# The output projection of a transformer block: retention rows, residual tiles and the gate in another place and order

## The chip, the cores and the metric

The kernel runs on one core of one Trainium2 chip. The metric is the device time of one execution in microseconds; for the kernel before it is 2900.07 us, the median of three runs (2897.08 to 2903.02).

## The reference

Two blocks are computed in float32. The change lies in the first, between its mixers and its feed-forward stage.

```python
# one block of the first stage (DEPTH = 1); D_MODEL = 1024, SEQ = 1024, D_FF = 4096
x = layer_norm(x, ln_in_g, ln_in_b)
mod = silu(c) @ w_ada + b_ada
sh1, sc1, gt1, sh2, sc2, gt2 = split(mod, 6)
h = x * (1.0 + sc1) + sh1
proj = h @ w_in                     # q_c, kv_c, k_r for the attention; r_q, r_k, r_v, r_g for the retention
a = mla_mixer(q_c, kv_c, k_r, ...)                  # 512 columns
r = retention_mixer(r_q, r_k, r_v, r_g, ...)        # 512 columns, 4 heads, a norm per row and head, a gate from r_g
y = concatenate([a, r], -1) @ w_out
x = layer_norm(ALPHA * x + gt1 * y, ln1_g, ln1_b)
h = x * (1.0 + sc2) + sh2
f = square(relu(h @ w_ff1)) @ w_ff2
x = layer_norm(ALPHA * x + gt2 * f, ln2_g, ln2_b)
# a second block follows (differential attention, gated linear attention, cross attention, mixture of experts)
```

## The kernel before

The sequence of 1024 rows is cut into eight tiles of 128 rows (t = 0 to 7), and for the matmuls into two halves of four tiles. Float32 products are made of three matmuls on pairs of a rounded value and its residual (hi and lo): mm3 (L194) issues hi x hi, hi x lo and lo x hi, one matmul each at L197, L198 and L199. A product of 128 rows, 1024 inner and 512 outer columns is 24 matmuls into one PSUM bank. Weights come as pieces of 128x1024 into a raw buffer (DMA, L160), ScalarE rounds them (L164, whi), DVE subtracts (L165, wlo). Three raw buffers and five pairs of hi and lo turn round; the output projection has three more pairs (xwh, xwl).

The order of each engine is set when the program is built: the code is written in the order below, and a scheduler then orders each engine's instructions by when their operands are expected and by the priority of the code's order. Buffers of a pool are handed on when their last reader is done, and a pool that opens where another closed waits for the last users of the old memory.

Before the change the stage runs as follows. retain (L820) walks the retention's eight tiles: loads of qk and v, transposes, the scan, the output rows r (L779), their statistics. After every fourth tile the statistics give a reciprocal root, and 16 activations on ScalarE (L795) norm four rows. Between the tiles gate_cols (L798) computes the gate's columns with the projection of the input, 24 matmuls each. ret_half (L809) transposes four rows (L250), applies the group gain on ScalarE (L815, u), the gate on DVE (L816) and splits the result into the left operand of the output projection (L817, L818); for rows 0 to 3 it stands after the sixth tile, for rows 4 to 7 at the end.

out_proj (L858) loads the gate gt1 over all partitions, and the gain and bias of the input norm (ling, linb), scaled by ALPHA on DVE (L866). For each tile it loads x, norms it (L869, DVE), multiplies by ling (L870, DVE) and adds linb (L871, POOL): that is the residual acc. gemm_resident (L212) multiplies with both column halves of w_out resident: tiles 0 to 3 for columns 0 to 511, the same tiles for columns 512 to 1023, then tiles 4 to 7 with both halves in turn. Four PSUM banks hold results; the evacuation multiplies by gt1 (L877, from PSUM, DVE) and adds to acc (L878, DVE). When a tile has both halves, done (L901) takes its statistics, norms it (L904, DVE), and after four tiles mod_half (L461) transposes them into the operand of the feed-forward stage, and POOL applies ALPHA times ln1's gain and bias to acc (L908, L909).

feed_forward (L917) has eight chunks of 512 hidden columns. In a chunk eight up products of 24 matmuls are followed by relu (ScalarE, L940), the square (DVE, L942), rounding (ScalarE, L943, hidh) and residual (DVE, L944); then 16 down products with weights that POOL has multiplied by gt2 (L996), which DVE adds to acc (L1007).

## Time and profile before

| what | value |
|---|---|
| median of three runs | 2900.07 us (2897.08 to 2903.02) |
| profiled execution | 2900.44 us |
| its span | 2898.6 us |
| mean granted clock of TensorE | 0.976 of full speed |
| TensorE, DVE, ScalarE, POOL busy | 95%, 63%, 47%, 16% of the span |
| stage of the change | some 430 to 735 us of the span |

Times are counted from the span's start. PE is TensorE, ACT is ScalarE, POOL is GpSimd, SP the engine that issues the loads. An idle time in brackets is that of the engine before the instruction, and the arrow names what ended it. Matmuls are pipelined, so the distance of two starts tells their pace, and not the duration that is printed. The granted clock is given in parts of full speed (2.4 GHz).

### The profile page before, as it was taken

The numbers are of one execution on the slowest core, as the hardware profiler recorded it, in microseconds if no ns is written. First come the engines' busy times: TensorE is split into PE (matmuls) and PEld (weight loads), VectorE is DVE, ScalarE is ACT, GpSimd is POOL, SyncE is SP. The second block draws the span as 40 slices with busy tenths as digits, with TensorE's granted clock in tenths as the row PEclk, the third lists the DMA queues.
The fourth block names the chain that finished last, engine by engine and source line by source line (L and its number), as shares of the span: only waits on it lengthen the run. The fifth ranks groups of instructions, "written<-read, shape, count | busy, mean of one in ns | idle before, by whom it ended". The sixth has DMA issues, their size and how long they took to land. (4 is left out here: it accounts for less than half of the span.)

```text
span 2898.6 us, 36767 instructions
## 1 busy us (share of the span) xinstructions
PE 2748.2 (95%) x13590; PEld 2177.6 (75%) x13590; DVE 1837.4 (63%) x3617; ACT 1354.5 (47%) x2319; POOL 473.9 (16%) x426
## 2 busy tenths in 40 slices
PE   7999999978999999999899999899999799999997
PEld 4876667756888888887686777688778688877776
DVE  6655753697534444435754766646555799988886
ACT  5644543413211221113534765624431588877786
POOL 0042201054100111102310010000003311111111
PEclk9999999988999999999999999899999899999999
DMA  8563434501211121111224212222235799999996
GB/s 292 173 201 116 114 97 128 179 6 63 62 44 37 59 59 51 44 44 51 93 81 133 85 56 87 84 108 102 66 120 197 279 360 350 348 344 347 351 350 210
DMA packets 245565, 432.54 MB, mean 149 GB/s; under 512 B 45540, under 2 KB 95108, under 8 KB 245000
## 3 DMA queue, kind: packets, MB, share of 16 engines
q1 hardware_dynamic: 225288, 377.69, 38.3%
q0 software_dynamic: 20096, 52.49, 5.7%
q8 instruction: 108, 1.77, 0.3%
q14 instruction: 73, 0.60, 0.1%
HBM read 380.79 MB, written 66.08 MB: 154 GB/s over the span
## 5 line engine op out<-in xcount | busy, mean ns | idle before, releaser
L1788 DVE TENSOR_TENSOR wdl<-w,wdh 128x1024 fp32r<-128x1024 f32 x384 | 457.8, 1221 | 60.5 <-ACT wdh L1787 55.6
L1787 ACT CAST wdh<-w 128x1024 fp32r<-128x1024 f32 x384 | 391.5, 1050 | 91.0 <-DMA w<-in_w_e_gate 25.3
L197 PE MATMUL mm<-whi,x 128*128 128x512 f32 (+1 forms) x1008 | 410.3, 407 | 20.9 <-DVE y L877 18.0
L198 PE MATMUL mm<-wlo,x 128*128 128x512 f32 (+1 forms) x1008 | 405.7, 403 | 4.7 <-DVE wlo L165 3.1
L199 PE MATMUL mm<-whi,x 128*128 128x512 f32 (+1 forms) x1008 | 404.2, 401 | 0.0
L164 ACT CAST whi<-raw 128x1024 fp32r<-128x1024 f32 (+1 forms) x111 | 114.0, 1043 | 401.6 <-PE m L199 264.5
L197 PEld LDWEIGHTS mm<-whi,x 128*128 128x128 f32 x1008 | 194.6, 193 | 59.8 <-DVE y L877 18.4
L197 PE MATMUL mm<-x,whi 128*128 128x512 f32 (+1 forms) x592 | 234.2, 396 | 4.1 <-ACT relu L940 3.3
L199 PE MATMUL mm<-x,wlo 128*128 128x512 f32 (+1 forms) x592 | 232.5, 393 | 0.0
L198 PE MATMUL mm<-x,whi 128*128 128x512 f32 (+1 forms) x592 | 232.4, 393 | 0.0
L165 DVE TENSOR_TENSOR wlo<-raw,whi 128x1024 fp32r<-128x1024 f32 (+1 forms) x111 | 155.2, 1405 | 121.4 <-ACT whi L164 121.0
L198 PEld LDWEIGHTS mm<-wlo,x 128*128 128x128 f32 x1008 | 193.9, 192 | 45.6 <-issue 5.7
L199 PEld LDWEIGHTS mm<-whi,x 128*128 128x128 f32 x1008 | 193.6, 192 | 37.0 <-issue 3.6
L1007 DVE TENSOR_TENSOR acc<-acc,m 128x512 f32<-128x512 f32 x128 | 87.9, 686 | 205.1 <-PE m L199 204.9
L199 PE MATMUL m<-whi,hidl 128*128 128x512 f32 x512 | 200.2, 391 | 0.0
L198 PE MATMUL m<-wlo,hidh 128*128 128x512 f32 x512 | 200.2, 391 | 0.0
L197 PE MATMUL m<-whi,hidh 128*128 128x512 f32 x512 | 200.2, 391 | 0.0
L996 POOL TENSOR_TENSOR raw<-raw,gt 128x1024 f32<-128x1024 f32 x32 | 85.6, 2686 | 517.7 <-DMA raw<-in_w_ff 517.7
L197 PEld LDWEIGHTS mm<-x,whi 128*128 128x128 f32 (+1 forms) x592 | 110.9, 187 | 30.1 <-ACT relu L940 3.9
L199 PEld LDWEIGHTS mm<-x,wlo 128*128 128x128 f32 (+1 forms) x592 | 110.8, 187 | 25.2
L198 PEld LDWEIGHTS mm<-x,whi 128*128 128x128 f32 (+1 forms) x592 | 111.0, 187 | 24.4
L594 ACT ACTIVATE e<-sc,nm 128x256 f32<-128x256 f32 (+6 forms) x128 | 96.5, 756 | 40.8 <-PE tp L671 17.7
(582 smaller groups left out, 5832.6 us busy)
## 6 DMA issues: line engine op xcount, KB each, us to landing
w<-in_w_e_gate SPq DMA_DIRECT2D x62, 1024.0 KB, 18.0
w<-in_w_e_up SPq DMA_DIRECT2D x62, 1024.0 KB, 17.5
w<-in_w_e_down SPq DMA_DIRECT2D x62, 1024.0 KB, 16.4
raw<-in_w_ff SPq DMA_DIRECT2D x64, 512.0 KB, 4.1
araw<-in_w_ada SPq DMA_DIRECT2D x24, 1024.0 KB, 7.0
raw<-in_w_in SPq DMA_DIRECT2D x36, 512.0 KB, 3.7
raw<-in_w_ckv SPq DMA_DIRECT2D x16, 512.0 KB, 6.8
x<-in_x SPq DMA_DIRECT2D x8, 512.0 KB, 7.2
```

The lines of the kernel that those rows point to most:

```text
L164: nc.scalar.copy(hi, raw)
L165: nc.vector.tensor_tensor(lo, raw, hi.bitcast(F32), op=ALU.subtract)
L197: mm(ps, lh, rh, start=start, stop=False)
L198: mm(ps, lh, rl, start=False, stop=False)
L199: mm(ps, ll, rh, start=False, stop=stop)
L594: nc.scalar.activation(e, ps, AF.Exp, bias=nm, accum_out=l)
L996: lambda raw: nc.gpsimd.tensor_tensor(raw, raw, gt, op=ALU.mult)) for f in range(4)]
L1007: nc.vector.tensor_tensor(acc[t][:, ns], acc[t][:, ns], ps, op=ALU.add)
L1787: nc.scalar.copy(wh, w)
L1788: nc.vector.tensor_tensor(wl, w, wh.bitcast(F32), op=ALU.subtract)
```

## The change

Retention rows are normed in pairs (ret_norm): two heads of a row on ScalarE, two on DVE. Rows 4 to 7, their gates and statistics lie in a pool of their own (keep) that stays open, and their assembly (second) is called behind the second product of the output projection, with one u buffer in place of two; the first half's assembly is called one tile earlier. The residual of tiles 0 to 2 is loaded and built during the retention, with full-width ling and linb; that of tiles 3 to 7 behind the projection's first product (rest), in column halves. Its norm is on ScalarE, gain and bias on DVE. The first column half of w_out is loaded during the retention. gt1 is multiplied in PSUM for the first column half and into the weights, on POOL, for the second. Tiles 4 to 7 run all of the first column half, then all of the second. acc is normed on ScalarE, and ln1's gain and bias are applied on DVE in the first chunk of the feed-forward stage.

```diff
-    def gemm_resident(self, p, psp, xt, w, evac):
+    def gemm_resident(self, p, psp, xt, w, evac, first=None, row=None, late=False, hooks=None):
         spare = [(self.tl(p, [P, 1024], F32R, tag=f"xwh{i}"), self.tl(p, [P, 1024], F32R, tag=f"xwl{i}")) for i in range(3)]
-        ws = [self.wchunk(w, 0, 512), self.wchunk(w, 512, 512, spare=spare)]
-        for c, t in [(c, t) for c in range(2) for t in range(4)] + [(c, t) for t in range(4, NT) for c in range(2)]:
+        if late:
+            rest = [(c, t) for c in range(2) for t in range(4, NT)]
+        else:
+            rest = [(c, t) for t in range(4, NT) for c in range(2)]
+        for n, (c, t) in enumerate([(c, t) for c in range(2) for t in range(4)] + rest):
             ps = self.tl(psp, [P, 512], tag="mm")
             for k in range(8):
                 self.mm3(ps, xt(t, k), ws[c][k], k == 0, k == 7)
             evac(c, t, ps)
+            if hooks and n in hooks:
+                hooks[n]()
...
-            if t % 4 == 3:
-                m = self.tl(p, [P, 4, 4], tag="m", bufs=2)
...
+            if t % 2:
+                norms.append(lambda t=t, mv=mv: self.ret_norm(keep, rows[t - 1:t + 1], mv))
+    def ret_norm(self, p, rows, mv):
+        nc = self.nc
+        m = self.tl(p, [P, 2, 4], tag="m", bufs=2)
+        nc.vector.tensor_scalar(m, mv[:, :, :, 1], EPS1, None, op0=ALU.add)
+        y = self.rsqrt(p, m.rearrange("p a b -> p (a b)"), 8, tag="rr").rearrange("p (a b) -> p a b", a=2)
+        b = self.tl(p, [P, 2, 4], tag="mb", bufs=2)
+        nc.vector.scalar_tensor_tensor(b, mv[:, :, :, 0], -1.0, y, op0=ALU.mult, op1=ALU.mult)
+        for j, r in enumerate(rows):
+            for h in range(4):
+                s = slice(h * P, (h + 1) * P)
+                if h < 2:
+                    nc.scalar.activation(r[:, s], r[:, s], AF.Identity, scale=y[:, j, h:h + 1], bias=b[:, j, h:h + 1])
+                else:
+                    nc.vector.tensor_scalar(r[:, s], r[:, s], y[:, j, h:h + 1], b[:, j, h:h + 1], op0=ALU.mult, op1=ALU.add)
...
-            u = self.tl(p, [P, 512], tag="u", bufs=2)
+            u = self.tl(p, [P, 512], tag="u", bufs=1)
...
+        def half_of(half, pst):
+            mix.append(self.xhalf(half))
+            self.mix_in(self.d_mla, mix[half], half, 0)
+            self.ret_half(keep, pst, rows[4 * half:4 * half + 4], g[half], mix[half], gb[:, 0], gb[:, 1])
+        def second(pst):
+            norms.pop()()
+            half_of(1, pst)
+        for t in self.retention(p, keep, psa, pst, rows, norms):
             half = t // 4
             self.gate_cols(p, psp, hv, wg, half, t % 4, g[half][:, t % 4])
-            if t % 4 == 3:
-                mix.append(self.xhalf(half))
-                self.mix_in(self.d_mla, mix[half], half, 0)
-            if t == 5:
-                self.ret_half(p, pst, rows[:4], g[0], mix[0], gb[:, 0], gb[:, 1])
-        self.ret_half(p, pst, rows[4:], g[1], mix[1], gb[:, 0], gb[:, 1])
-        return mix
+            if t % 2 and t < NT - 1:
+                norms.pop()()
+            if t == 4:
+                half_of(0, pst)
+            between(t)
+        return mix, second
...
+    def out_setup(self, p, c, width):
+        nc = self.nc
+        r = [self.tl(p, [P, width], tag=n) for n in ("ling", "linb")]
+        for x, n in zip(r, ("ln_in_g", "ln_in_b")):
+            nc.sync.dma_start(x, self.brow(n, D)[:, c * width:(c + 1) * width])
+            nc.scalar.mul(x, x, ALPHA)
+        return r
+    def out_norm(self, acc, t):
+        nc = self.nc
+        nc.sync.dma_start(acc[t], self.a["x"][t * P:(t + 1) * P])
+        nc.scalar.activation(acc[t], acc[t], AF.Identity, scale=self.lnr[:, t:t + 1], bias=self.lnb[:, t:t + 1])
+    def out_gain(self, z, gain, bias):
+        self.nc.vector.tensor_tensor(z, z, gain, op=ALU.mult)
+        self.nc.vector.tensor_tensor(z, z, bias, op=ALU.add)
...
-        g, b = [self.tl(p, [P, D], name=n) for n in ("ling", "linb")]
-        for x, n in ((g, "ln_in_g"), (b, "ln_in_b")):
-            nc.sync.dma_start(x, self.brow(n, D))
-            nc.vector.tensor_scalar(x, x, ALPHA, None, op0=ALU.mult)
-        for t in range(NT):
-            nc.sync.dma_start(acc[t], self.a["x"][t * P:(t + 1) * P])
-            nc.vector.tensor_scalar(acc[t], acc[t], self.lnr[:, t:t + 1], self.lnb[:, t:t + 1], op0=ALU.mult, op1=ALU.add)
-            nc.vector.tensor_tensor(acc[t], acc[t], g, op=ALU.mult)
-            nc.gpsimd.tensor_tensor(acc[t], acc[t], b, op=ALU.add)
         def evac(c, t, ps):
-            s = slice(c * 512, (c + 1) * 512)
-            z = acc[t][:, s]
-            y = self.tl(p, [P, 512], tag="y", bufs=2)
-            nc.vector.tensor_tensor(y, ps, gt[:, s], op=ALU.mult)
-            nc.vector.tensor_tensor(z, z, y, op=ALU.add)
+            z = acc[t][:, c * 512:(c + 1) * 512]
+            if c == 0:
+                nc.vector.tensor_tensor(ps, ps, gt[:, :512], op=ALU.mult)
+            nc.vector.tensor_tensor(z, z, ps, op=ALU.add)
             if c:
                 done(t)
-        self.gemm_resident(p, psp, mix, self.a["w_out"], evac)
+        self.gemm_resident(p, psp, mix, self.a["w_out"], evac, first=first, row=gt, late=True, hooks=hooks)
...
-            nc.vector.tensor_scalar(z, z, r, nb, op0=ALU.mult, op1=ALU.add)
+            nc.scalar.activation(z, z, AF.Identity, scale=r, bias=nb)
             if t % 4 == 3:
+                hv.append(self.xhalf(t // 4))
                 self.mod_half(p, pst, acc[t - 3:t + 1], hv[t // 4], a2, b2)
-                for y in acc[t - 3:t + 1]:
-                    nc.gpsimd.tensor_tensor(y, y, g, op=ALU.mult)
-                    nc.gpsimd.tensor_tensor(y, y, b, op=ALU.add)
...
+            def gain_bias(n, by=None):
+                r = [self.tl(p, [P, D], tag=x) for x in ("lng", "lnb")]
+                for x, y in zip(r, "gb"):
+                    nc.sync.dma_start(x, self.brow(f"{n}_{y}", D))
+                    if by:
+                        nc.scalar.mul(x, x, by)
+                return r
+            g1, b1 = gain_bias("ln1", ALPHA)
...
+                    if c == 0:
+                        nc.vector.tensor_tensor(acc[t], acc[t], g1, op=ALU.mult)
+                        nc.vector.tensor_tensor(acc[t], acc[t], b1, op=ALU.add)
...
+        EARLY = 3
+        with self.pool("acce", side="right") as accp, ExitStack() as late:
+            acc = [self.tl(accp, [P, D], name=f"acc{t}") for t in range(EARLY)]
+            with self.pool("retk", side="right") as keep:
+                with self.pool("ret") as p, self.pool("retps", bufs=2, space=PSUM) as psp, \
+                        self.pool("rett", bufs=2, space=PSUM) as pst, self.pool("reta", space=PSUM) as psa:
+                    lin = self.out_setup(p, 0, D)
+                    first = []
+                    def between(t):
+                        if t < EARLY:
+                            self.out_norm(acc, t)
+                            self.out_gain(acc[t], *lin)
+                        elif t == NT - 2:
+                            first.append(self.wchunk(self.a["w_out"], 0, 512))
+                    mix, second = self.retain(p, keep, psp, psa, pst, hv, between)
+                accp = late.enter_context(self.pool("accl"))
+                acc += [self.tl(accp, [P, D], name=f"acc{t}") for t in range(EARLY, NT)]
+                with self.pool("wo") as wp, self.pool("wops", bufs=4, space=PSUM) as psp, self.pool("wopt", bufs=3, space=PSUM) as pst:
+                    hv = []
+                    def rest():
+                        for t in range(EARLY, NT):
+                            self.out_norm(acc, t)
+                        for c in range(2):
+                            lin = self.out_setup(wp, c, 512)
+                            for t in range(EARLY, NT):
+                                self.out_gain(acc[t][:, c * 512:(c + 1) * 512], *lin)
+                    self.out_proj(wp, psp, self.xt_of(mix), acc, first[0], self.after_mix(wp, pst, hv, acc),
+                                  {0: rest, 1: lambda: second(pst)})
```

The first place is TensorE's order at the projection's start. Before, the transposes of rows 4 to 7 (tp from r) end like this, and the first product (mm) follows:

```order
L250 MATMUL tp_5549<-ident,r_5180 128x128 [waits Activation_49]
L250 MATMUL tp_5549<-ident,r_5259 128x128
L250 MATMUL tp_5549<-ident,r_5378 128x128
L250 MATMUL tp_5549<-ident,r_5434 128x128
L250 MATMUL tp_5559<-ident,r_5180 128x128 [waits Activation_49]
L250 MATMUL tp_5559<-ident,r_5259 128x128
L250 MATMUL tp_5559<-ident,r_5378 128x128
L250 MATMUL tp_5559<-ident,r_5434 128x128
L197 MATMUL mm_5697<-whi_5656,x_1238_5141 128x512
L198 MATMUL mm_5697<-wlo_5657,x_1238_5141 128x512
```

In the changed kernel the last gate product is followed by six transposes of two rows, and then by the first product:

```order
L199 MATMUL mm_5554<-x_183_798,wlo_4766 128x512
L258 MATMUL tp_5771<-ident,r_5216 128x128 [waits PE_49,Activation_49]
L258 MATMUL tp_5771<-ident,r_5345 128x128 [waits Activation_49]
L258 MATMUL tp_5781<-ident,r_5216 128x128 [waits Activation_49]
L258 MATMUL tp_5781<-ident,r_5345 128x128
L258 MATMUL tp_5791<-ident,r_5216 128x128
L258 MATMUL tp_5791<-ident,r_5345 128x128
L197 MATMUL mm_5639<-whi_5503,x_1266_5267 128x512
L198 MATMUL mm_5639<-wlo_5504,x_1266_5267 128x512
```

The transposes of the fourth column group of all four rows stand within the third product:

```order
L197 MATMUL mm_5811<-whi_5509,x_1266_5267 128x512
L198 MATMUL mm_5811<-wlo_5510,x_1266_5267 128x512
L199 MATMUL mm_5811<-whi_5509,x_1267_5268 128x512
L258 MATMUL tp_5801<-ident,r_5216 128x128 [waits Activation_49]
L258 MATMUL tp_5801<-ident,r_5345 128x128
L258 MATMUL tp_5801<-ident,r_5451 128x128
L258 MATMUL tp_5801<-ident,r_5531 128x128 [waits DVE_49]
L197 MATMUL mm_5811<-whi_5509,x_1266_5267 128x512
```

The first two products stand between the two pairs of rows now, and the fourth group (tp_5801) waits for ScalarE in the middle of a product.

The second place is ScalarE's order there. Before, the norms (L795) are followed by u (L815) and casts of weights:

```order
L795 ACTIVATE r_5259<-r_5259,mb_5473,rry_5461 128x128 x4
L795 ACTIVATE r_5378<-r_5378,mb_5473,rry_5461 128x128 x4
L795 ACTIVATE r_5434<-r_5434,mb_5473,rry_5461 128x128 [waits Activation_49]
L795 ACTIVATE r_5434<-r_5434,mb_5473,rry_5461 128x128 x3
L707 CAST x_1314_5519<-raw_5525 128x1024 [waits DMAHW1_49]
L815 ACTIVATE u_5534<-tp_5529,gnh 128x512 [waits PE_49]
L815 ACTIVATE u_5544<-tp_5539,gnh 128x512 [waits PE_49]
L164 CAST whi_5668<-raw_5667 128x1024 [waits DMAHW5_49]
L817 CAST x_1314_5519<-u_5534 128x512 [waits DVE_49]
```

In the changed kernel u (L829) stands behind three casts of weights and four residual norms (L894):

```order
L164 CAST whi_5618<-raw_5617 128x1024 [waits Pool_49]
L164 CAST xwh_1346_5611<-raw_5624 128x1024 [waits Pool_49]
L164 CAST xwh_1348_5613<-raw_5629 128x1024 [waits DMAHW4_49,DMAHW3_49,DMAHW5_49,DMAHW2_49,DMAHW6_49,DMAHW1_49,Pool_49]
L894 ACTIVATE acc_5589<-acc_5589,lnb,lnr 128x1024 [waits DMAHW6_49]
L894 ACTIVATE acc_5590<-acc_5590,lnb,lnr 128x1024 [waits DMAHW7_49]
L894 ACTIVATE acc_5591<-acc_5591,lnb,lnr 128x1024 [waits DMAHW0_49,DMASW3_49,DMASW2_49]
L894 ACTIVATE acc_5592<-acc_5592,lnb,lnr 128x1024 [waits DMAHW1_49]
L829 ACTIVATE u_5776<-tp_5771,gnh 128x512 [waits PE_49]
L164 CAST xwh_1350_5615<-raw_5634 128x1024 [waits Pool_49]
L894 ACTIVATE acc_5593<-acc_5593,lnb,lnr 128x1024 [waits DMAHW3_49]
L888 ACTIVATE ling_5676<-ling_5676 128x512 [waits DMAHW4_49]
```

The casts wait for POOL now, and u, which waits for TensorE alone, stands behind them.

The third place is POOL's order from the retention's end on. Before, it adds linb to acc, and applies ln1 to it:

```order
L871 TENSOR_TENSOR acc_5580<-acc_5580,linb 128x1024
L871 TENSOR_TENSOR acc_5581<-acc_5581,linb 128x1024
L871 TENSOR_TENSOR acc_5582<-acc_5582,linb 128x1024
L871 TENSOR_TENSOR acc_5583<-acc_5583,linb 128x1024
L908 TENSOR_TENSOR acc_5576<-acc_5576,ln1g 128x1024
L908 TENSOR_TENSOR acc_5577<-acc_5577,ln1g 128x1024
L909 TENSOR_TENSOR acc_5576<-acc_5576,ln1b 128x1024
L909 TENSOR_TENSOR acc_5577<-acc_5577,ln1b 128x1024
```

In the changed kernel four weight pieces are multiplied by gt1, and then those of the feed-forward stage by gt2 (L1028):

```order
L757 TENSOR_TENSOR kzpad_4779<-qk_5423,zt 128x2x2x64
L177 TENSOR_TENSOR raw_5617<-raw_5617,gt_5609 128x1024
L177 TENSOR_TENSOR raw_5624<-raw_5624,gt_5609 128x1024
L177 TENSOR_TENSOR raw_5629<-raw_5629,gt_5609 128x1024
L177 TENSOR_TENSOR raw_5634<-raw_5634,gt_5609 128x1024
L1028 TENSOR_TENSOR raw_6812<-raw_6812,gt_6523 128x1024
L1028 TENSOR_TENSOR raw_6819<-raw_6819,gt_6523 128x1024
```

All operations on acc have left POOL; on DVE those of ln1 stand among the squares (L974), the residuals (L976) and the weight residuals (L165) of the first chunk, as here:

```order
L165 TENSOR_TENSOR wlo_6821<-raw_6819,whi_6820 128x1024
L976 TENSOR_TENSOR hidl<-sq_6715,hidh 128x512
L1037 TENSOR_TENSOR acc_5589<-acc_5589,lnb_6526 128x1024
L1036 TENSOR_TENSOR acc_5590<-acc_5590,lng_6525 128x1024
L1036 TENSOR_TENSOR acc_5591<-acc_5591,lng_6525 128x1024
L974 TENSOR_TENSOR sq_6746<-relu_6744 128x512
L165 TENSOR_TENSOR wlo_6828<-raw_6826,whi_6827 128x1024
L976 TENSOR_TENSOR hidl<-sq_6746,hidh 128x512
L1037 TENSOR_TENSOR acc_5590<-acc_5590,lnb_6526 128x1024
```

Two full-width operations stand there for nearly every square.

## Rows read from the trace of the kernel before

**Rows 1.** Stretches: busy us (instructions) of PE, PEld, DVE, ACT, POOL, clock, DMA share, GB/s.
```profile
520.00:540.00 20.00, 17.40 (x97) 14.42 (x96) 14.06 (x44) 9.96 (x19) 0.00 (x0) 1.00 0.08 27
540.00:560.00 20.00, 16.24 (x60) 12.61 (x61) 12.39 (x18) 16.32 (x27) 0.00 (x0) 0.74 0.60 193
560.00:580.00 20.00, 20.00 (x90) 16.45 (x89) 16.16 (x15) 0.03 (x1) 5.91 (x3) 1.00 0.99 345
580.00:600.00 20.00, 2.63 (x12) 1.83 (x10) 20.00 (x12) 0.00 (x0) 14.68 (x5) 0.64 0.06 15
```

**Rows 2.** TensorE in order of time: start, us, instruction, idle time before it.
```profile
536.36 0.39 PE L199 MATMUL mm<-x,wlo 128*128 128x512 f32 x1
...
546.13 1.97 PE L250 MATMUL tp<-ident,r 128*128 128x128 f32 x8 [1.90 <-ACT u L815]
547.75 0.78 PE L197 MATMUL mm<-whi,x 128*128 128x512 f32 x1
...
551.71 0.40 PE L197 MATMUL mm<-whi,x 128*128 128x512 f32 x1
```

**Rows 3.** TensorE in order of time, around 600 us.
```profile
600.64 0.79 PE L197 MATMUL mm<-whi,x 128*128 128x512 f32 x1 [18.00 <-DVE y L877]
...
606.32 0.39 PE L198 MATMUL mm<-xwl,x 128*128 128x512 f32 x1
```

**Rows 4.** TensorE in order of time, around 672 us.
```profile
672.03 1.75 PE L250 MATMUL tp<-ident,acc 128*128 128x128 f32 x7 [8.67 <-DVE acc L904]
673.44 0.77 PE L197 MATMUL mm<-x,whi 128*128 128x512 f32 x1
...
677.85 0.45 PE L198 MATMUL mm<-x,whi 128*128 128x512 f32 x1
```

**Rows 5.** TensorE in order of time, around 710 us.
```profile
705.87 0.39 PE L199 MATMUL mm<-x,wlo 128*128 128x512 f32 x1
709.59 0.79 PE L197 MATMUL mm<-x,whi 128*128 128x512 f32 x1 [3.33 <-ACT relu L940]
...
715.30 0.48 PE L198 MATMUL mm<-x,whi 128*128 128x512 f32 x1
```

**Rows 6.** ScalarE in order of time, around 708 us.
```profile
708.42 0.62 ACT L943 CAST hidh<-sq 128x512 fp32r<-128x512 f32 x1 [12.93 <-POOL acc L909]
```

**Rows 7.** DVE in order of time, 571 to 601 us.
```profile
571.78 3.32 DVE L870 TENSOR_TENSOR acc<-acc,ling 128x1024 f32<-128x1024 f32 x1
...
575.75 2.90 DVE L878 TENSOR_TENSOR acc<-acc,y 128x512 f32<-128x512 f32 x1
...
599.90 1.28 DVE L877 TENSOR_TENSOR y<-mm,gt 128x512 f32<-128x512 f32 x2
```

**Rows 8.** Groups by line, 430 to 740 us: count, busy us, mean ns, idle time before.
```profile
L871 POOL TENSOR_TENSOR acc<-acc,linb 128x1024 f32<-128x1024 f32 x8 | 22.9, 2878 | 69.4 <-DVE acc L870 69.4
...
L909 POOL TENSOR_TENSOR acc<-acc,ln1b 128x1024 f32<-128x1024 f32 x8 | 21.2, 2673 | 0.0
L165 DVE TENSOR_TENSOR wlo<-raw,whi 128x1024 fp32r<-128x1024 f32 x17 | 20.8, 1222 | 14.7 <-ACT whi L164 14.4
...
L164 ACT CAST whi<-raw 128x1024 fp32r<-128x1024 f32 x17 | 17.8, 1049 | 34.2 <-PE mm L199 18.2 <-DMA raw<-in_w_ff 11.4 <-DMA raw<-in_w_out 3.0
...
L996 POOL TENSOR_TENSOR raw<-raw,gt 128x1024 f32<-128x1024 f32 x4 | 10.5, 2640 | 6.1 <-DMA raw<-in_w_ff 6.1
...
L815 ACT ACTIVATE u<-tp,gnh 128x512 f32<-128x512 f32 x8 | 5.8, 773 | 0.7 <-DVE x L818 0.6
```

**Rows 9.** Groups by line, ScalarE, the whole execution.
```profile
L438 ACT ACTIVATE x<-x,lnb,lnr 128x1024 f32<-128x1024 f32 x8 | 9.5, 1233 | 4.1 <-DVE lnb L435 4.1
```

**Rows 10.** DMA issues, 430 to 740 us: count, KB each, median us to landing.
```profile
raw<-in_w_out SPq DMA_DIRECT2D x8, 512.0 KB, 4.6
...
qk<-d_rqk SPq DMA_DIRECT2D x8, 256.0 KB, 3.2
...
gt<-d_gt SPq DMA_DIRECT2D x2, 512.0 KB, 10.0
```

More of the change, by code (lines that the diff above doesn't have):

```diff
@@ L708, in mix_in, with retention @@
             nc.vector.tensor_tensor(lo[:, k], raw, hi[:, k].bitcast(F32), op=ALU.subtract)
-    def retention(self, p, psa, pst, rows):
+    def retention(self, p, keep, psa, pst, rows, norms):
         nc, a = self.nc, self.a
@@ L753, in retention @@
         for t in range(NT):
-            if t % 4 == 0:
-                mv = self.tl(p, [P, 4, 4, 2], tag="mv", bufs=2)
+            if t % 2 == 0:
+                mv = self.tl(keep, [P, 2, 4, 2], tag="mv", bufs=2)
             if t + 1 < NT:
@@ L783, in retention @@
                 nc.vector.bn_stats(bst, r[:, h * P:(h + 1) * P])
[L784 to L796 removed]
+                nc.vector.bn_aggr(mv[:, t % 2, h], bst)
+            if t % 2:
+                norms.append(lambda t=t, mv=mv: self.ret_norm(keep, rows[t - 1:t + 1], mv))
+            yield t
+    def ret_norm(self, p, rows, mv):
[12 more added lines that the diff above has]
+                    nc.vector.tensor_scalar(r[:, s], r[:, s], y[:, j, h:h + 1], b[:, j, h:h + 1], op0=ALU.mult, op1=ALU.add)
     def gate_cols(self, p, psp, hv, ws, half, f, out):
@@ L818, in ret_half, with retain @@
             nc.vector.tensor_tensor(mix[1][:, 4 + h], u, mix[0][:, 4 + h].bitcast(F32), op=ALU.subtract)
-    def retain(self, p, psp, psa, pst, hv):
+    def retain(self, p, keep, psp, psa, pst, hv, between):
         nc = self.nc
-        rows, mix = [], []
-        gb = self.tl(p, [P, 2, 4], name="gnh")
+        rows, mix, norms = [], [], []
+        gb = self.tl(keep, [P, 2, 4], name="gnh")
         for i, n in enumerate(("ret_gn_g", "ret_gn_b")):
@@ L827, in retain @@
         wg = self.wchunk(self.a["w_in"], 1440, 512)
-        g = [self.tl(p, [P, 4, 512], name=f"gates{i}") for i in range(2)]
-        for t in self.retention(p, psa, pst, rows):
+        g = [self.tl(x, [P, 4, 512], name=f"gates{i}") for i, x in enumerate((p, keep))]
+        def half_of(half, pst):
[6 more added lines that the diff above has]
+        for t in self.retention(p, keep, psa, pst, rows, norms):
             half = t // 4
             self.gate_cols(p, psp, hv, wg, half, t % 4, g[half][:, t % 4])
-            if t % 4 == 3:
-                mix.append(self.xhalf(half))
-                self.mix_in(self.d_mla, mix[half], half, 0)
-            if t == 5:
-                self.ret_half(p, pst, rows[:4], g[0], mix[0], gb[:, 0], gb[:, 1])
-        self.ret_half(p, pst, rows[4:], g[1], mix[1], gb[:, 0], gb[:, 1])
-        return mix
+            if t % 2 and t < NT - 1:
[4 more added lines that the diff above has]
+        return mix, second
     def gates(self, p, psp, hv, w, c0, tiles, first, keep=None):
@@ L856, in gate_rows, with out_proj @@
         self.mix_rows(pst, r, mix, t, 4, gain)
-    def out_proj(self, p, psp, mix, acc, done):
+    def out_setup(self, p, c, width):
[12 more added lines that the diff above has]
+        self.nc.vector.tensor_tensor(z, z, bias, op=ALU.add)
+    def out_proj(self, p, psp, mix, acc, first, done, hooks):
         nc = self.nc
@@ L1917, in run @@
                     self.project_in(ip, ap, psp, hv, ci)
-        with self.pool("ret") as p, self.pool("retps", bufs=2, space=PSUM) as psp, \
-                self.pool("rett", bufs=2, space=PSUM) as pst, self.pool("reta", space=PSUM) as psa:
-            mix = self.retain(p, psp, psa, pst, hv)
-        with self.pool("acc") as accp:
-            acc = [self.tl(accp, [P, D], name=f"acc{t}") for t in range(NT)]
-            with self.pool("wo") as wp, self.pool("wops", bufs=4, space=PSUM) as psp, self.pool("wopt", bufs=3, space=PSUM) as pst:
-                hv = self.xhalves()
-                self.out_proj(wp, psp, self.xt_of(mix), acc, self.after_mix(wp, pst, hv, acc))
+        EARLY = 3
```

24 lines of the change are left out of this document (3 added, 21 removed).

## The prediction

> **What bounds the kernel now.** I read the page first: TensorE is busy for 95% of the span, so a change pays only where TensorE stands still or is clocked down. The stretches of 20 us show where that is inside the part that the change touches: from 540 TensorE is busy for 16.24 us at a mean granted clock of 0.74, from 560 it is full, and from 580 it is busy for 2.63 us at 0.64 [rows 1]. TensorE's order of time then gives four pauses, each followed by matmuls at the lower of the two clock levels (1.2 instead of 2.4 GHz). Such a matmul takes 0.44 us (nine of them between 547.75 and 551.71 [rows 2]), so 0.22 us at the full level: a slow matmul loses half of its time.
>
> Pause 1 [rows 2]: after the last gate product TensorE transposes retention rows 4 to 7 as ScalarE's norms hand them over, then waits for ScalarE's u. From the last product's start at 536.36 to the first matmul of the output projection at 547.75 are 11.39 us, less 0.22 for that product and about 1.9 for the 16 transposes (eight of them ran in 1.62) makes 9.3; the nine slow matmuls add 2.0. Loss 11.3.
> Pause 2 [rows 3]: 18.00 us for DVE's gate product (L877), then 13 slow matmuls in 5.68, half of which is 2.8. Loss 20.8.
> Pause 3 [rows 4]: 8.67 us for DVE's norm of an acc tile (L904), then ten slow matmuls in 4.41, half 2.2, and about 0.3 on the slow transposes. Loss 11.2.
> Pause 4 [rows 5]: 3.33 us for ScalarE's relu, then 13 slow matmuls in 5.71, half 2.85. Loss 6.2. Behind it stands ScalarE's hidh cast, which had idled 12.93 us for POOL's ln1 bias (L909) [rows 6].
> Sum 49.5 us. That is all that the change can take back.
>
> **What makes the pauses 2 to 4.** While POOL adds linb to an acc tile, DVE's operations on two SBUF operands stretch: the gain product L870 took 3.32 us at 571.78 and the accumulation L878 2.90 at 575.75, while L877, whose input lies in PSUM, took 0.64 each [rows 7]. DVE therefore reached the evacuations that free TensorE's PSUM banks 18 us late, and the backlog reaches into pause 3.
>
> **Part 1, retention rows kept open.** The output projection now begins with tiles 0 and 1 (48 products, 48 x 0.22 = 10.6 us) while the norms of rows 6 and 7 run, half of them on DVE. Only six transposes of rows 4 and 5 stand before them, and their norms lie before the last gate product in the order. So pause 1 goes, 11.3 us. Call E the end of the last gate product.
> What is late next: after nine products of the third tile TensorE's order holds the four transposes of the fourth column group, and these need the first u, since three transpose banks exist. TensorE is there at E + 0.6 + 57 x 0.22 + 12 transposes of 0.1, so about E + 14.3. In ScalarE's order that u stands behind two casts that wait for POOL's multiplication of weights by gt1, and behind four norms of residual tiles. The chain: gt1's load is issued behind the last w_out pieces at about E + 2.8 (it takes memory of the retention and stands behind two loads that wait for DVE to release a buffer); a w_out piece took 4.6 us to land, and gt1 took 10.0 from its issue [rows 10], so it lands at E + 7.4 to E + 12.8. POOL multiplies three pieces at 2.64 to 2.88 [rows 8]: 7.9 to 8.6. Then ScalarE: a cast of 1.05 and u of 0.77 [rows 8], and four norms of 1.23, by the norm of the same shape at the kernel's start [rows 9]: 6.7. u is there at E + 22.0 to E + 28.1, and TensorE waits 7.7 to 13.8 us, with a spell of slow matmuls behind it as after the other pauses (2.0 to 2.8). I take gt1 near the w_out row, because ahead of it stand two pieces and not seven: 7.9 + 2.1 = 10.0 us, bounds 0 (if gt1 lands so early that the casts are ready) and 16.6.
>
> **Part 2, retention's start.** Before the first qk load, SP's queue now holds three x tiles, one w_out piece, ling and linb: six transfers of 512 KB, 3.1 MB, which at the 345 GB/s of the full stretch [rows 1] are 9 us; a qk load itself took 3.2 us to landing [rows 10]. The gate products don't depend on them and TensorE has those to work on between the scans, so I take 2.3 us, bounds 0 and 9. The new norm and gain of tiles 0 to 2 lie on ScalarE and DVE, which have idle time there (DVE was busy for 14.06 of 20 us just before pause 1) [rows 1].
>
> **Part 3, the residual and the gate.** POOL's eight additions of 2.88 [rows 8] go; norm goes to ScalarE, gain and bias to DVE. Eight multiplications of weights take their place: four, on POOL. For columns 0 to 511 the gate is multiplied in PSUM: 0.64 us as in L877 [rows 7], in the same place, so nothing is added; for the other half it falls away, 8 x 0.64 us less on DVE. Pause 2 goes. What is late next is DVE's queue: between E and E + 52 it has norms, weight residuals, u products, ten half-width gain and bias operations and the first eight evacuations, 41.6 us by the durations of rows like L165 (1.22) and L877. The evacuation that frees the fifth bank falls at about E + 46, where TensorE arrives at E + 44.6: 2 us, bounds 0 and 11. The 11 is four POOL multiplications of 2.7 us that block DVE as in rows 7.
> The Trainium skill, "SBUF — State Buffer", section "Who interferes with whom", says that a vector instruction with two SBUF inputs contends with a GpSimd instruction that reads SBUF, and one with at most one SBUF input doesn't. The trace agrees (2.90 against 0.64 us). By it the PSUM evacuations stay free of POOL, and only the gain, bias and weight residuals are held, which would put the sum nearer to the upper bound if they fall under POOL's four multiplications, some 8 us above my forecast.
>
> **Part 4, assembling behind the second product.** Tiles 4 to 7 now run all first columns and then all second, and acc tiles are normed on ScalarE, off DVE. Pause 3 was the DVE backlog; without it what is left is the chain of one tile from evacuation to norm, against products of the next tile, 24 x 0.22 = 5.3 us each. The chain is some twelve small operations, about 6 us. I leave 1.5 us for acc6 and acc7 and 1.5 for the ScalarE norms of acc3 on which the first accumulations wait: 3, bounds 0 and 11.2 (pause 3 stays).
>
> **Part 5, ln1 gain and bias to DVE.** POOL's sixteen operations (L909's eight took 21.2 us [rows 8]) become sixteen on DVE inside the first ff chunk, 16 x 1.22 = 19.5 us. Pause 4 goes with POOL's. Between the projection's last product and the first down product TensorE has eight up products of 24 x 0.22 and the transposes, some 46 us; DVE has there the residuals of the last four tiles (some 9 us), then 15 operations of 0.64 and 20 of 1.22, 34.0 us, so it is as full as TensorE. POOL's four multiplications by gt2 (L996, 2.64) lie in the same stretch. I count 4 us of wait for the last weight residual and the first evacuation, bounds 0 and 10.6 (4 x 2.64 blocked).
>
> **Sum.** 49.5 - (10.0 + 2.3 + 2 + 3 + 4 = 21.3) = 28.2 us saved. The profiled execution took 2900.44 us (1.84 around its span of 2898.6), 0.37 above the median of 2900.07, which I neglect: 2872.
>
> **Rivals.**
> Full recovery: ScalarE's chain for u is hidden (gt1 lands early) and DVE keeps up; left are 2.3 + 3 and 1 or 2 besides, 7 us: 2858. For it: DVE's evacuations from PSUM are short. Against it: three POOL multiplications alone are 7.9 us and stand ahead of u.
> DVE becomes the bound: it takes POOL's work of the residual and of ln1, and POOL's remaining multiplications block it. Retention 2.3, u 10, evacuations 11, tiles 3, ff 10.6, together 36.9: saved 12.6, 2888. For it: rows 7. Against it: DVE loses eight gate products and the contention of 24 POOL operations.
> No change: one of the big pauses stays under another name, for instance 18 us while u waits for gt1 as long as in the trace of before and pause 3 remains: 16.6 + 2.3 + 11 + 11.2 + 4 = 45: 2896 to 2904.
> Slower: retention's start. SP issues in order, and the third x tile there waits for the last store of the attention output; ada's weights, ling, linb, qk and v stand behind it. Each us beyond what the gate products cover goes to the end one for one. It decides when retention ends over 28 + 6 = 34 us later, for example when the six loads and the scans' loads in turn wait for buffers: 2910. Against it: 9 us is all that the bytes ask.
>
> **How the numbers follow.** Forecast 0.58 (its own range 2865 to 2880), full recovery 0.17, DVE bound 0.15, no change 0.04, slower 0.06. Differences under 0.2% (6 us) can't be told from none. Faster 0.58 + 0.17 + 0.15 = 0.90, same 0.04, slower 0.06. For 8 in 10 the range takes the forecast, most of full recovery and most of the DVE case: 2855 to 2890.
>
> **What would show it.** Right: TensorE goes from the last gate product to the projection without a gap over 1 us; a single pause of 8 us and more stands before the transposes of the fourth group, put down to ScalarE's u, and ScalarE's time before it is POOL's multiplications; no 18 us pause; the ff chunk's first products follow the projection within 2 us; busy DVE around the end of the first up products. Wrong: TensorE's pause before u is absent, or POOL's multiplications end 10 us later than E + 16; a pause put down to an acc evacuation of over 5 us; the last gate product ending more than 5 us later than 536.6.

## The result, and the profile after

The changed kernel takes 2868.80 us (median of four runs, 2867.14 to 2870.24), the kernel before 2898.57 us in the same comparison (2894.22 to 2903.02): a ratio of 0.9899 with a 95% interval of 0.9883 to 0.9914. That is 29.8 us less where 28.2 were forecast; the interval reaches from 24.9 to 33.9 us, so the two are not told apart.

TensorE's order of time in the changed kernel answers to [rows 2 to 5] (start, us, instruction, idle time before it):

```profile
538.14 0.39 PE L199 MATMUL mm<-x,wlo 128*128 128x512 f32 x1
538.37 0.82 PE L258 MATMUL tp<-ident,r 128*128 128x128 f32 x6
538.95 0.48 PE L197 MATMUL mm<-whi,x 128*128 128x512 f32 x1
...
552.41 0.39 PE L199 MATMUL mm<-whi,x 128*128 128x512 f32 x1
561.58 1.11 PE L258 MATMUL tp<-ident,r 128*128 128x128 f32 x4 [8.78 <-ACT u L829]
562.35 0.78 PE L197 MATMUL mm<-whi,x 128*128 128x512 f32 x1
...
565.48 0.39 PE L198 MATMUL mm<-wlo,x 128*128 128x512 f32 x1
...
696.64 0.50 PE L198 MATMUL m<-wlo,hidh 128*128 128x512 f32 x1 [2.75 <-DVE wlo L165]
...
703.58 0.50 PE L197 MATMUL m<-whi,hidh 128*128 128x512 f32 x1 [0.76 <-DVE acc L1043]
```

Pause 1 is gone: from the last gate product (538.14) to the projection's first matmul (538.95) lie 0.81 us with six transposes in them. So are pauses 2 to 4: from 538 to 735 the three idle times shown are the only ones above 0.3 us, and 8.78 us for u is the one that the forecast named. Behind it seven matmuls run at the lower level (562.35 to 565.48, 0.45 us each). The pause of 2.75 us at 696.64 has none behind it.

ScalarE's order of time in the changed kernel shows why u is late:

```profile
542.22 1.65 ACT L808 ACTIVATE r<-r,mb,rry 128x128 f32<-128x128 f32 x4 [3.05 <-DVE mb L803]
549.63 1.05 ACT L164 CAST whi<-raw 128x1024 fp32r<-128x1024 f32 x1 [5.76 <-POOL raw L177]
552.00 1.05 ACT L164 CAST xwh<-raw 128x1024 fp32r<-128x1024 f32 x1 [1.32 <-POOL raw L177]
555.28 1.04 ACT L164 CAST xwh<-raw 128x1024 fp32r<-128x1024 f32 x1 [2.23 <-POOL raw L177]
556.23 4.63 ACT L894 ACTIVATE acc<-acc,lnb,lnr 128x1024 f32<-128x1024 f32 x4
560.77 0.76 ACT L829 ACTIVATE u<-tp,gnh 128x512 f32<-128x512 f32 x1
```

POOL's, and DVE's first wait for gt1:

```profile
547.20 8.05 POOL L177 TENSOR_TENSOR raw<-raw,gt 128x1024 f32<-128x1024 f32 x3 [34.04 <-DMA gt<-d_gt]
...
547.13 0.70 DVE L910 TENSOR_TENSOR mm<-mm,gt 128x512 f32<-128x512 f32 x1 [3.79 <-DMA gt<-d_gt]
```

gt1 was issued at 540.30 and landed just before 547.13, when DVE's first gate product in PSUM stopped waiting for it. POOL multiplies three pieces from 547.20 to 555.25 (8.05 us), the third cast ends at 556.32, four residual norms take 4.63 us, and u starts at 560.77. Every link of the forecast's chain is there, in its size.

For a measure that leaves out jitter in the parts that are the same in all kernels, I take the time from a common event ahead of the change (TensorE's wait for DVE's adab, 459.22 us in the trace of before, 457.69 in that of after) to DVE's last accumulation in the feed-forward stage, called the stage below; like the trace it is that of one execution. The group of these accumulations (ns shortest, median, longest; first and last start in us) in the trace of before:

```profile
L1007 DVE TENSOR_TENSOR acc<-acc,m x128: 672/687/690, 734.0 to 1403.2; 128x512 f32<-128x512 f32 x128
```

And in the trace of after:

```profile
L1043 DVE TENSOR_TENSOR acc<-acc,m x128: 670/687/689, 702.9 to 1370.0; 128x512 f32<-128x512 f32 x128
```

The last of 128 accumulations starts at 1403.2 before and at 1370.0 after. The stage is 944.0 us before and 912.3 after: 31.7 less. The part behind it was 1495.4 and 1498.4 us; in the twelve profiles of this study it lies between 1492 and 1500 whatever the kernel is.

The stage has scatter of its own. In the nine kernels with three early residual tiles the code up to the last gate product reads the same, and that product ends 79.15 to 80.95 us behind the common event; from the first accumulation to the last the twelve profiles have 667.1 to 669.2 us. So I don't tell stages apart that differ by less than some 4 us (an estimate: the sum of the two spreads, 1.8 and 2.1).

### The profile page after: what moved, and what is told of

It reads as the page before. It is cut to its first block, busy times and chain, and to the rows that moved or that the text cites. A ratio compares the mean times of both kernels' runs of the same rounds, so it can differ in the third digit from the quotient of the medians.

```text
span 2868.4 us, 36818 instructions
## 1 busy us (share of the span) xinstructions
PE 2738.4 (95%) x13590; PEld 2169.9 (76%) x13590; DVE 1819.0 (63%) x3665; ACT 1373.6 (48%) x2327; POOL 420.9 (15%) x406
## 5 line engine op out<-in xcount | busy, mean ns | idle before, releaser
L165 DVE TENSOR_TENSOR wlo<-raw,whi 128x1024 fp32r<-128x1024 f32 (+1 forms) x111 | 162.1, 1468 | 126.7 <-ACT whi L164 126.1
L1028 POOL TENSOR_TENSOR raw<-raw,gt 128x1024 f32<-128x1024 f32 x32 | 86.7, 2724 | 632.1 <-DMA raw<-in_w_ff 527.2
```

Source lines behind the costliest of these rows:

```text
L165: nc.vector.tensor_tensor(lo, raw, hi.bitcast(F32), op=ALU.subtract)
L1028: lambda raw: nc.gpsimd.tensor_tensor(raw, raw, gt, op=ALU.mult)) for f in range(4)]
```

## The experiments

All but one start from the changed kernel (stage 912.3 us, 2868.80 us).

**e4_linb_dve: what made pause 2.** The kernel before, one line changed.

```diff
-            nc.gpsimd.tensor_tensor(acc[t], acc[t], b, op=ALU.add)
+            nc.vector.tensor_tensor(acc[t], acc[t], b, op=ALU.add)
```

> The kernel before with one line changed: the addition of linb (128x1024, eight times) on DVE in place of POOL. Theory A (pause 2 is contention: under POOL's additions DVE's norm, gain and accumulation of acc took 14.4 + 11.7 + 18.0 us where 6.5 + 9.8 + 11.0 stand alone, some 14 us too many in the pause's stretch): DVE gets 8 x 1.22 = 9.8 us more work and loses about 14 us of contention; pause 2 shrinks from 18 to some 14 us, 2893 to 2896. Rival B (no contention, DVE is simply full): the pause grows by the 9.8 us, 2906 to 2909.

Measured 2891.30 us against 2898.39 for the kernel before in that comparison, ratio 0.998 (0.9969 to 0.999), stage 934.5 us. DVE in order of time:

```profile
589.63 0.81 DVE L869 TENSOR_SCALAR acc<-acc,lnr,lnb 128x1024 f32<-128x1024 f32 x1
590.35 1.22 DVE L871 TENSOR_TENSOR acc<-acc,linb 128x1024 f32<-128x1024 f32 x1
...
592.62 0.68 DVE L878 TENSOR_TENSOR acc<-acc,y 128x512 f32<-128x512 f32 x1
```

And TensorE:

```profile
595.70 0.79 PE L197 MATMUL mm<-whi,x 128*128 128x512 f32 x1 [12.36 <-DVE y L877]
```

With eight operations more on DVE the pause is shorter, 12.36 us for 18.00: DVE's operations have their undisturbed times (1.22 and 0.68 us, where [rows 7] had 3.32 and 2.90). The norm (L869), which reads one tile and two values per row, has its own too; in the trace of before it took 2.82 us while POOL added:

```profile
593.28 2.82 DVE L869 TENSOR_SCALAR acc<-acc,lnr,lnb 128x1024 f32<-128x1024 f32 x1
```

The contention is shown, rival B falls. Theory A was too cautious: it expected a pause of some 14 us and 2893 us or more. DVE took on 9.8 us of work and was ready 5.6 us earlier, so the contention had cost it some 15 us ahead of that pause (an estimate from these two numbers). The 12.36 us left are DVE's own residual work: it has no idle time from 569.67, its first norm, to the gate product that ends the pause. The change starts this work earlier.

**e2_gate_dve: what holds u.** The gate in PSUM for both column halves.

```diff
-            if c == 0:
-                nc.vector.tensor_tensor(ps, ps, gt[:, :512], op=ALU.mult)
+            nc.vector.tensor_tensor(ps, ps, gt[:, c * 512:(c + 1) * 512], op=ALU.mult)
...
-        self.gemm_resident(p, psp, mix, self.a["w_out"], evac, first=first, row=gt, late=True, hooks=hooks)
+        self.gemm_resident(p, psp, mix, self.a["w_out"], evac, first=first, late=True, hooks=hooks)
```

> The changed kernel with the gate multiplied in PSUM on DVE for both column halves, nothing of it in the weights on POOL. Theory A (the chain gt1, POOL, ScalarE's casts holds u): the casts wait for their loads alone, u is ready some 7 us earlier, the pause before the fourth group falls from 8.8 us to 0 to 3 us, and DVE has 8 x 0.69 us more, which hides: 2858 to 2864. Rival B (DVE is the bound of the stage): the pause falls, but evacuations come late by about 5 us and TensorE waits for a PSUM bank: 2864 to 2868. Rival C (the four residual norms in front of u, not POOL, cost the pause): pause 5 us or more, 2865 or above.

Measured 2860.97 us (2859.98 to 2861.91), stage 906.6. TensorE in order of time:

```profile
554.40 0.72 PE L258 MATMUL tp<-ident,r 128*128 128x128 f32 x4 [1.90 <-ACT u L829]
```

And ScalarE:

```profile
549.80 3.88 ACT L894 ACTIVATE acc<-acc,lnb,lnr 128x1024 f32<-128x1024 f32 x3 [0.23 <-DMA acc<-in_x]
553.59 0.76 ACT L829 ACTIVATE u<-tp,gnh 128x512 f32<-128x512 f32 x1
```

The pause falls to 1.90 us, and no evacuation holds TensorE. POOL's multiplications are what held u; what is left of the pause stands behind three residual norms (3.88 us). Eight gate products more on DVE (0.69 us each) hide. In the feed-forward stage's first chunk TensorE waits 3.02 us for the last weight residual (690.33), with eight slow matmuls behind it. Theory A.

**e1_banks: the bank alone.**

```diff
-                with ..., self.pool("wopt", bufs=3, space=PSUM) as pst:
+                with ..., self.pool("wopt", bufs=4, space=PSUM) as pst:
```

> The changed kernel with a fourth PSUM bank for the transposes of the output projection, so that the fourth group's transposes need no u before them. Theory A (the forecast's: u, behind POOL's multiplications and the residual norms, costs TensorE 8.8 us and some 1.9 us of slow matmuls, but only because three banks exist): the pause at the fourth group goes. But the four u are still made one after the other on ScalarE and DVE, and the last residual of the second half (DVE L832) ended at 588.7 us in the changed kernel; TensorE would now want it at the first product of tile 4, some 45 us behind the last gate product, at about 584. So a new pause of 3 to 5 us there: 2862 to 2866. Rival B (the banks alone were short): no new pause, 10.5 us less: 2858. Rival C (the order has some other wait there): 2868 to 2870.

Measured 2872.22 us (2869.21 to 2875.22), stage 913.9. The pause at the fourth group is gone, and a longer one stands before the seventh product:

```profile
585.94 0.79 PE L197 MATMUL mm<-whi,x 128*128 128x512 f32 x1 [10.22 <-DVE acc L911]
```

DVE in that stretch:

```profile
575.90 3.10 DVE L898 TENSOR_TENSOR acc<-acc,ling 128x512 f32<-128x512 f32 x5 [0.49 <-ACT ling L888]
579.79 3.10 DVE L899 TENSOR_TENSOR acc<-acc,linb 128x512 f32<-128x512 f32 x5 [0.79 <-ACT linb L888]
...
585.21 1.27 DVE L911 TENSOR_TENSOR acc<-acc,mm 128x512 f32<-128x512 f32 x2
```

None of the three was right in its number. A named the right side (something late comes next), but the wrong wait: not the operand of tile 4, but the evacuation of the third and fourth products (585.21). C's condition came (another wait in the order), and its 2868 to 2870 lies at the lower end of the runs. The evacuation stands in DVE's queue behind twenty half-width gain and bias operations: the first ten wait for ling and linb, which ScalarE scales behind the same casts and norms as u (566.30), and the other ten for the second halves of ling and linb, which are loaded into the same buffers when the first ten have read them. TensorE's pause for u had covered DVE's lateness, and both hang on the casts that wait for POOL. So the 10 us of the u pause are not to be had by letting TensorE pass it; e2_gate_dve, which frees the casts, has the same evacuation 6.8 us earlier (118.2 us behind the common event, for 125.0) and gains 5.7 us of the stage.

**e8_both: gate on DVE and the fourth bank.** The two diffs above together.

> The gate on DVE for both halves (e2_gate_dve) and the fourth PSUM bank for transposes (e1_banks) together. e2_gate_dve keeps a pause of 1.90 us for u with 8 slow matmuls, together 3.5 us. Theory A (behind it stands DVE's queue: the evacuation of the third product ends at 577.2 us there, and TensorE needs its bank at 579.3, 2 us of slack): 3.5 us go and some 1.5 us with or without slow matmuls come back, 0.5 to 2 us faster than e2_gate_dve: 2859 to 2860.5. Rival B (nothing behind it): 2857.5.

Measured 2860.51 us (2859.82 to 2864.14), stage 906.4 against 906.6: the pause for u is gone, and TensorE waits 2.46 us for an evacuation at 577.75, and 3.64 in place of 3.02 for the last weight residual of the first chunk. Rival B falls. Theory A had the new wait, somewhat shorter; that the kernel is any faster than e2_gate_dve is not shown.

**e12_early1: how much room DVE has.** `EARLY = 1` in place of 3.

> The changed kernel with one residual tile built during the retention in place of three; tiles 1 and 2 join the others behind the first product. Theory A (DVE's queue stands right behind the pause for u: the evacuation of the fourth product ends at 583.1 us, and TensorE needs the bank of the third and fourth at about 583.6): 8 more half-width operations, 4.9 us, come ahead of it, so a new pause of 3 to 5 us with slow matmuls at the seventh product, 2873 to 2877, while the start of the retention gets 0.5 to 1.5 us shorter. Rival B (DVE has room): 2867 to 2869.5.

Measured 2876.14 us (2873.68 to 2877.67), stage 920.1. TensorE in order of time:

```profile
590.12 0.79 PE L197 MATMUL mm<-whi,x 128*128 128x512 f32 x1 [6.49 <-DVE acc L911]
```

A pause of 6.49 us at the seventh product with matmuls at the lower level behind it: theory A, longer than its 3 to 5. The residual of tiles 1 and 2 must be built early. In the changed kernel the same place had half a microsecond to spare (the third product's evacuation is the first of these two, and the seventh product starts behind it):

```profile
582.51 1.28 DVE L911 TENSOR_TENSOR acc<-acc,mm 128x512 f32<-128x512 f32 x2
583.78 0.40 PE L197 MATMUL mm<-whi,x 128*128 128x512 f32 x1
```

The last gate product ends 78.8 us behind the common event, for 80.7. That is not clear of the 79.15 to 80.95 of the kernels with three early tiles, so what the two tiles cost the retention is not shown.

**e6_first: rows 4 to 7 ahead of the first product.**

```diff
                     hv = []
+                    second(pst)
...
-                                  {0: rest, 1: lambda: second(pst)})
+                                  {0: rest})
```

> The changed kernel with the assembly of rows 4 to 7 called ahead of the projection's first product, not behind its second. In its order the transposes of rows 6 and 7 stand within the first product and those of the fourth group near the start of the second. Theory A (the forecast's: the two products in front cover the norms of rows 6 and 7, worth 11.3 us of pause 1): TensorE waits for the norms some 2 us and for u, which stands behind one cast that waits for POOL, until 13 us behind the last gate product, about 6 us: together 8 us, the same as the pause that goes. 2866 to 2872, no change. Rival B (the place behind the second product is what pays): pause 1 comes back, 2876 to 2880.

Measured 2872.10 us (2870.82 to 2873.49), stage 913.0. TensorE in order of time:

```profile
546.77 0.48 PE L258 MATMUL tp<-ident,r 128*128 128x128 f32 x2 [2.05 <-DVE r L810]
...
551.87 0.66 PE L258 MATMUL tp<-ident,r 128*128 128x128 f32 x4 [0.31 <-ACT u L829]
...
593.04 0.47 PE L258 MATMUL tp<-ident,acc 128*128 128x128 f32 x1 [3.20 <-ACT acc L931]
```

Pause 1 doesn't come back, because the scheduler puts most of the first product ahead of the transposes of rows 6 and 7; TensorE waits 2.05 us for their norms and then 3.20 and twice 0.66 for acc's norms at 593. The pause for u is traded for smaller ones with slow matmuls behind them, as theory A had it in sum, at its upper edge; in its parts it was wrong, since u cost 0.31 us and not 6, and acc's norms come late instead. What the call's place behind the second product is worth is not shown: the stages differ by 0.7 us, the medians by 3.3, and the intervals of the two ratios overlap (0.9894 to 0.9927 here). So pause 1 went because products stand before the transposes of rows 6 and 7; the norms in pairs, half of them on DVE, went with it, and no run takes them back.

**e5_pairs: the order of tiles 4 to 7.** `late=False`.

> The changed kernel with the old order of tiles 4 to 7 in the projection: both column halves of a tile in turn, not all first and then all second halves. Theory A (pause 3 was DVE's backlog, which is gone; the chain of one tile, about 6 us, hides beside the next products in either order): the same within 1.5 us, 2867.5 to 2870.5. Rival B (the new order is what removed pause 3): TensorE waits before the transposes of tiles 4 to 6 for 4 to 9 us, 2874 to 2880.

Measured 2868.72 us (2865.45 to 2873.54), stage 911.9, the same pauses (8.40, 2.90, 0.74). Theory A: once DVE's backlog is gone, the order of the tiles makes no difference that can be seen.

**e3_ln1_pool: ln1 back on POOL.**

```diff
-                        nc.vector.tensor_tensor(acc[t], acc[t], g1, op=ALU.mult)
-                        nc.vector.tensor_tensor(acc[t], acc[t], b1, op=ALU.add)
+                        nc.gpsimd.tensor_tensor(acc[t], acc[t], g1, op=ALU.mult)
+                        nc.gpsimd.tensor_tensor(acc[t], acc[t], b1, op=ALU.add)
```

> The changed kernel with the sixteen ln1 operations of the first feed-forward chunk back on POOL, in the same place in the code. In the changed kernel they cost TensorE 2.75 + 0.76 us of waits there, since DVE is full (20.00 of 20 us from 680). Theory A (POOL's sixteen operations of 2.7 us, 43 us behind its four multiplications by gt2, hold DVE's squares and residuals as in the kernel before, where two squares took 5.68 us): the wait doesn't go, it moves to the squares; 2868 to 2876. Rival B (DVE's load alone counts): the 3.5 us go, 2864 to 2866.

Measured 2877.05 us (2875.26 to 2881.29), stage 921.6. TensorE in order of time:

```profile
695.79 0.50 PE L197 MATMUL m<-whi,hidh 128*128 128x512 f32 x1 [2.65 <-ACT whi L164]
700.24 0.79 PE L198 MATMUL m<-wlo,hidh 128*128 128x512 f32 x1 [3.94 <-DVE wlo L165]
...
712.48 0.79 PE L197 MATMUL m<-whi,hidh 128*128 128x512 f32 x1 [3.76 <-DVE acc L1043]
```

Three pauses, 10.35 us, for 3.5, with 17 slow matmuls behind the last two: theory A's side, 1 us above its range, and in the down products rather than at the squares. POOL is busy for 20.00 and 19.92 of 20 us from 680, and DVE's squares and weight residuals stretch:

```profile
691.27 2.87 DVE L974 TENSOR_TENSOR sq<-relu 128x512 f32<-128x512 f32 x1
...
696.83 3.35 DVE L165 TENSOR_TENSOR wlo<-raw,whi 128x1024 fp32r<-128x1024 f32 x1
```

In the trace of the changed kernel:

```profile
690.76 0.68 DVE L974 TENSOR_TENSOR sq<-relu 128x512 f32<-128x512 f32 x1
...
695.37 1.21 DVE L165 TENSOR_TENSOR wlo<-raw,whi 128x1024 fp32r<-128x1024 f32 x1
```

Without ln1's operations DVE is busy for 34.66 of the 40 us from 680, and with them, undisturbed, for 29.90. Keeping ln1 off POOL is worth 9.3 us of the stage.

**e9_split and e10_best: ln1 of tiles 0 to 3 earlier.** On e2_gate_dve, and on e8_both.

```diff
+            if t == 3:
+                for c in range(2):
+                    g, b = [self.tl(p, [P, 512], tag=x) for x in ("ling", "linb")]
+                    for x, n in ((g, "ln1_g"), (b, "ln1_b")):
+                        nc.sync.dma_start(x, self.brow(n, D)[:, c * 512:(c + 1) * 512])
+                        nc.scalar.mul(x, x, ALPHA)
+                    for y in acc[:4]:
+                        self.out_gain(y[:, c * 512:(c + 1) * 512], g, b)
...
-                    if c == 0:
+                    if c == 0 and t >= 4:
```

> e2_gate_dve, and ln1's gain and bias of tiles 0 to 3 applied in the projection stage, behind their transposes (in column halves, 16 operations of 0.65 us), not in the first feed-forward chunk. Theory A (DVE is full in that chunk by the 19.5 us of ln1, and idle for 4 to 10 of 20 us between 600 and 660): with half of it gone, the 3.02 us wait for the last weight residual and its 8 slow matmuls go, 4.7 us in all: 2855.5 to 2857.5. Rival B (DVE's queue is as full during the projection): a new wait for a PSUM bank of 2 to 4 us there, 2859 to 2862.

> All three: gate on DVE, the fourth bank, ln1 of tiles 0 to 3 in the projection stage. Theory A (the terms add): e9_split less what e8_both gains on e2_gate_dve: 2854 to 2857. Rival B (DVE's queue in the projection decides for both): no faster than e9_split.

e9_split: 2858.11 us (2852.46 to 2861.17), ratio to before 0.9855 (0.9835 to 0.9874), stage 899.8, 6.8 less than e2_gate_dve. In the stretches (length, then busy us of TensorE, its weight loads, DVE, ScalarE, POOL, then the granted clock) the wait of the first chunk is gone:

```profile
680.00:700.00 20.00, 20.00 (x90) 16.55 (x89) 12.88 (x17) 6.13 (x9) 0.00 (x0) 1.00 0.46 138
```

The wait and its eight slow matmuls are 4.7 us of the 6.8, as theory A had it. The rest can't come from what was changed: 1.4 us lie before the last gate product, where the two kernels have the same code, and eight slow matmuls (1.75 us) are missing behind the pause for u, which is nearly as long as in e2_gate_dve (1.71 and 1.90 us). TensorE is earlier by that and waits 1.33 us for an evacuation at 576.94, of rival B's kind but smaller. The median moved 2.9 us, with the runs spread over 8.7, and settles neither. e10_best: 2858.40 us (2856.45 to 2860.92), stage 903.3: rival B, the fourth bank adds nothing that can be seen (3.14 us of wait for an evacuation at 576.55). e9_split has the lowest median, 10.7 us below the changed kernel; e10_best is not told apart from it.

## Why the prediction was right

- **The pauses of before.** 49.5 us were to be had; what new waits cost in the trace of after is 17.8 (below), so 31.7 by the sum, and the stage is 31.7 us shorter. That the two agree to a tenth is luck, given the scatter of the stage; that they agree within it is the mechanism.
- **u (10.0).** 8.78 us of idle time, seven slow matmuls (half of 3.13, 1.6) and slow transposes (0.3): 10.7. TensorE stood ready 14.4 us behind the end of the last gate product (14.3 forecast), and u was there at 23.2 (22.0 to 28.1). gt1 landed 6.8 us from its issue, between the two rows I had (4.6 and 10.0), POOL took 8.05, ScalarE 6.3 from there to the end of u (6.7 forecast). The prediction's text speaks of two casts behind POOL where the order has three; its sum goes by three pieces, so nothing hangs on it. But the term's meaning was incomplete: e1_banks shows that the pause hid DVE's lateness, so letting TensorE pass it gains nothing as long as the casts behind POOL hold DVE's work too.
- **Retention (2.3).** The last gate product ended 80.7 us behind the common event in after and 77.4 before (536.36 and one product's 0.23, against 459.22): 3.3. Over the nine kernels with this start it is 1.8 to 3.6, and no run shows which of the early loads and operations costs it.
- **Evacuations in the projection (2).** 0 in the trace of after. The queue was there, with half a microsecond to spare, as e12_early1 and e1_banks show. The DVE rival had the right resource: 4.9 us more work ahead of that evacuation cost 6.49 us of pause, of the 11 it had set.
- **Tiles 4 to 7 (3).** 0.3 (a wait for acc's norm); the order that the term spoke of makes no difference that can be seen (e5_pairs).
- **First chunk (4).** 2.75 + 0.76 us for the last weight residual and the first accumulation, the two waits named. With half of ln1's work taken off DVE the waits go (e9_split), and with POOL doing it they grow (e3_ln1_pool). But ln1's 19.5 us are not all of DVE's load: while POOL multiplies by gt2 (664.64 to 677.13), four DVE operations take 7.7 us more than undisturbed, two of them these:

```profile
670.85 3.42 DVE L1036 TENSOR_TENSOR acc<-acc,lng 128x1024 f32<-128x1024 f32 x1
674.79 3.42 DVE L1037 TENSOR_TENSOR acc<-acc,lnb 128x1024 f32<-128x1024 f32 x1
678.13 1.22 DVE L1036 TENSOR_TENSOR acc<-acc,lng 128x1024 f32<-128x1024 f32 x1
```

DVE then works without a gap up to the weight residual that TensorE waits for. So the contention with gt2 alone is longer than the wait of 2.75 us; no run takes it away, and the share of the two causes stays open.

The terms came to 21.3 and were 17.8. The two waits set inside the projection, 5 us, came to 0.3; u and the retention, 12.3 us, came to 14.0, which hides a third of that error. The rule of the Trainium skill ("SBUF — State Buffer", section "Who interferes with whom") would have put the sum 8 us higher if DVE's operations fell under POOL's multiplications. They did in part: three weight residuals took 6.83 us for 3 x 1.22.

```profile
550.72 2.33 DVE L165 TENSOR_TENSOR wlo<-raw,whi 128x1024 fp32r<-128x1024 f32 x1 [2.17 <-ACT whi L164]
553.08 4.50 DVE L165 TENSOR_TENSOR xwl<-raw,xwh 128x1024 fp32r<-128x1024 f32 x2
```

But TensorE stood before u from 552.80 to 561.58, and no wait for a weight residual shows in the projection. The Trainium skill limits its clause on instructions with at most one SBUF input, in the same section, to those outside VectorE's two-port modes, and the prediction left that out. For one such instruction the clause as the prediction had it is wrong here: the norm L869 has one such tile and stretched from 0.81 to 2.82 us (e4_linb_dve).

## What to carry to other kernels

An operation moved between VectorE and GpSimd is not priced by its own duration: 9.8 us more on VectorE made the kernel 7 us faster by the medians, and 19.5 us taken off it made it 8 us slower, because GpSimd's operations stretched those of VectorE that read two SBUF operands (3.35 us for 1.21), and the norm as well, while those with an operand in PSUM kept their time ([rows 7]). And a pause that the trace puts down to one engine can cover another that is as late: before spending effort on it, add what the next in line would then wait for, here by following the queue of the evacuations, and look for the wait that both stand behind, here POOL's multiplications.

## What was not expected

A pause and its slow matmuls don't go together by length: behind 2.75 us (696.64) the matmuls kept the full level, behind 1.90 us (e2_gate_dve, 554.40) eight ran at the lower:

```profile
554.82 0.74 PE L197 MATMUL mm<-whi,x 128*128 128x512 f32 x1
...
558.32 0.39 PE L199 MATMUL mm<-whi,x 128*128 128x512 f32 x1
```

Nor does the place decide: behind 1.71 us at the same transposes e9_split has none, and behind 2.73 us before the same weight residual as 696.64 e6_first has eight:

```profile
698.32 0.79 PE L198 MATMUL m<-wlo,hidh 128*128 128x512 f32 x1 [2.73 <-DVE wlo L165]
...
701.84 0.39 PE L197 MATMUL m<-whi,hidh 128*128 128x512 f32 x1
```

So a forecast can't tell the 1.75 us of such a spell for a pause of this size, and the difference of two kernels in one profile each may hold one. And the part behind the stage, the same in all kernels, varied by 8 us between profiles, as much as most of the differences tested here; the stage's length leaves that out, and has the smaller scatter given above.
